# A row-wise maximum norm: the first tail tile loaded as 8192 + 8192 columns instead of 12672 + 3712

## The chip, the cores and the metric

The kernel runs on one core of one Trainium2 chip. The metric is the device time of one execution in microseconds (us). TensorE is not used; the work is done by transfers from the chip's memory (16 DMA engines of the core, fed from the queue that SyncE, SP, issues into) and by VectorE (DVE in the profile), which reduces.

## The reference

```python
x = np.random.randn(8192, 8192).astype(np.float32)

def reference(x):
    return np.linalg.norm(x, ord=np.inf, axis=1)
```

For a matrix and `axis=1` this is the vector norm of every row: the largest absolute value in each of the 8192 rows. The input is 268 MB of float32, the output 8192 numbers. Every element is read once and takes part in one maximum.

## The kernel before, in words

**Tiles.** A tile in the on-chip memory has 128 partitions. Each partition holds two rows of the matrix that follow each other in memory, so 2 x 8192 = 16384 columns, 64 KB a partition and 8.4 MB a tile. The matrix makes 32 such tiles. The first 24 are the bulk, the last 8 the tail. Three buffers (`BUFS = 3`) go round: tile n is loaded into the buffer that tile n - 3 leaves. A buffer is released as a whole, when the last reduction that reads it has ended.

**Bulk (lines 300 to 307).** Each tile is one load on SP's queue and one reduction on VectorE, which takes the maximum of absolute values over each of the two rows and writes two numbers a partition to `r_bulk`. VectorE's instruction is issued from the helper `absmax` (line 296), so all reductions stand under L296 in the profile; they are told apart by the tile written: `r_bulk`, `part`, `t` or `r_tail`.

**Tail, first seven tiles (lines 309 to 320).** Here a tile is loaded in several pieces, so that VectorE can begin on a piece while the next is still coming. The table `TAIL` (line 18) gives the widths of the pieces, tile by tile; they are counted from 0 here, so that "tile 0" is the first line of `TAIL`, "tile 3" the fourth. The widths are written out by hand. `segments` (line 39) cuts the pieces at the end of a row, since a reduction has one row's maximum as its result: a piece that runs over the border between the two rows at column 8192 gets two reductions. Each reduction writes one number a partition to `part`, in the next free column of its row; `part` has room for three a row (`k_max`, line 283) and is set to zero by POOL at the start. For tile 0 the pieces 12672 and 3712 give three reductions: columns 0 to 8192 (row 0), 8192 to 12672 (4480 columns of row 1), both after the first load, and 12672 to 16384 (3712 columns of row 1) after the second.

**The last tile (lines 327 to 358).** It is loaded in twelve pieces (`LAST`, line 29) that get narrower, reduced one by one; one reduction over all of `part` (192 ns in the profile) makes the results of the first seven tail tiles in between. The bulk's results are stored from ScalarE's queue, those of the tail from SP's.

**What sets the order.** All loads are issued by SP in the order of the program (lines 303, 315, 341), each as soon as its buffer is free; there are eight completion semaphores, used in turn, so a load also waits until the load eight before it has landed. The DMA engines work through the queue in order. VectorE runs its reductions in the order of the program, each waiting for the load that it reads. Some functions at the end of the program take out waits that are implied by others, issue the first load ahead of the start, and close the program from POOL (lines 52 to 248); the change does not touch them.

Of the kernel before, what the change touches and what calls it, by code (L numbers as in the profile page):

```python
# [15 lines left out]


TAIL = [
    [12672, 3712],
    [4992, 11392],  # L20
    [7040, 9344],
    [9344, 7040],
# [372 lines left out]
```

## Time and profile before

| what | value |
|---|---|
| device time, three runs | 627.03, 626.57, 627.04 us; median 627.03 us |
| profiled execution, first to last instruction (span) | 624.1 us |
| last store of the profiled execution lands, from the span's start | 624.7 us |
| instructions | 151, of these 63 reductions on VectorE |
| VectorE busy | 552.4 us, 89% of the span |
| the load queue's packets, share of 16 DMA engines | 99.7% |
| bytes read | 268.44 MB, 430 GB/s over the span |

The profiled execution has no device time of its own beside its span; the three runs' median stands 2.9 us above the span.

How to read it: the span is the time from the first to the last instruction of one profiled execution, and all times of instructions and landings are counted from its start. "Busy" is the time in which an engine worked; "idle before" is the time that it stood still ahead of a group of instructions, and "<-" names what ended the wait. A load's "landing" is the moment at which all of it has arrived. Reductions overlap at their ends: the next one's start is recorded some 0.08 us before the end of the one in front, so what a reduction costs VectorE is read from start to start, not from its own duration.

In the tail the trace has, in us from the span's start:

| load of tail tile | columns | issued | landed | its first reduction starts |
|---|---|---|---|---|
| 0, first | 12672 | 445.24 | 481.59 | 483.82 |
| 0, second | 3712 | 445.61 | 485.97 | 497.14 |
| 1, first | 4992 | 464.55 | 491.89 | 501.06 |
| 1, second | 11392 | 464.92 | 505.38 | 506.32 |
| 2, first | 7040 | 483.93 | 513.70 | 518.31 |
| 2, second | 9344 | 484.30 | 524.70 | 525.70 |
| 3, first | 9344 | 501.18 | 535.73 | 535.75 |
| 3, second | 7040 | 501.55 | 544.11 | 545.61 |
| 6, first | 4096 | 553.12 | 587.83 | 587.85 |
| last tile, twelfth | 768 | 611.38 | 622.19 | 622.34 |

The load ahead of tile 0's, of the last bulk tile, landed at 466.66, and that tile's reduction ran from 466.68 to 483.90.

### The profile page before, as it was taken

How to read it: one execution, taken by the hardware profiler on the slowest of the kernel's cores; microseconds unless marked ns; L12 is line 12 of the kernel's file. 1: busy time of each engine (PE TensorE's matmuls, PEld its weight loads, DVE VectorE, ACT ScalarE, POOL GpSimd, SP SyncE). 2: the span in 40 equal slices, each digit the busy share in tenths (PEclk: the TensorE clock that was granted, in tenths of full speed). 3: DMA queues.
4: the chain of work that ended last, by engine and by line, in shares of the span. 5: the costliest groups of instructions: out<-in, count | busy, mean ns of one | idle time of the engine just before them, and what ended most of it. 6: DMA issues, size and time to landing. Idle time of an engine off the chain costs nothing.

```text
span 624.1 us, 151 instructions
## 1 busy us (share of the span) xinstructions
DVE 552.4 (89%) x63; POOL 0.3 (0%) x5
## 2 busy tenths in 40 slices
DVE  0688988889988899888898888988889999999999
POOL 0000000000000000000000000000000000000000
DMA  9999999999999999999999999999999999999998
GB/s 403 470 403 454 420 428 445 403 470 403 470 403 441 433 403 470 403 470 403 470 403 470 403 462 412 437 437 403 470 434 397 440 448 422 422 437 430 429 427 354
DMA packets 8593, 268.47 MB, mean 430 GB/s; under 512 B 1424, under 2 KB 1424, under 8 KB 2832
## 3 DMA queue, kind: packets, MB, share of 16 engines
q1 hardware_dynamic: 8064, 268.44, 99.7%
q10 hardware_dynamic: 528, 0.02, 0.1%
q14 instruction: 1, 0.01, 0.0%
HBM read 268.44 MB, written 0.03 MB: 430 GB/s over the span
## 4 chain that ended last, share of the span: by engine, by line
DMA 63%; DVE 36%; another core or an unknown queue 0%; DVEq 0%; issue 0%
DMA t<-in_x_dram 63%; DVE r_bulk L296 25%; DVE part L296 8%; DVE t L296 3%; DVEq L390 0%; DVE r_tail L296 0%
## 5 line engine op out<-in xcount | busy, mean ns | idle before, releaser
L296 DVE TENSOR_REDUCE r_bulk<-t 128x2 f32<-128x16384 f32 x24 | 413.3, 17220 | 70.6 <-DMA t<-in_x_dram 70.6
L296 DVE TENSOR_REDUCE part<-t 128x1 f32<-128x8192 f32 (+19 forms) x26 | 121.3, 4741 | 0.3
L296 DVE TENSOR_REDUCE t<-t 128x1 f32<-128x1792 f32 (+7 forms) x10 | 16.3, 1692 | 0.0
L296 DVE TENSOR_REDUCE r_tail<-t 128x1 f32<-128x772 f32 (+1 forms) x2 | 1.8, 948 | 0.0
L296 DVE TENSOR_REDUCE r_tail<-part 128x14 f32<-128x42 f32 x1 | 0.2, 192 | 0.0
L293 POOL MEMSET part<- 128x42 f32 x1 | 0.1, 133 | 0.0
L379 POOL MEMSET const-bfloat16-1.0<- 128x1 bf16 x1 | 0.1, 101 | 0.0
L379 POOL MEMSET const-uint8-127<- 128x1 uint8 x1 | 0.1, 101 | 0.0
L379 POOL MEMSET const-float32-0.0<- 128x1 f32 x1 | 0.1, 98 | 0.2 <-issue 0.2
L379 POOL MEMSET const-float32-1.0<- 128x1 f32 x1 | 0.1, 98 | 0.0
## 6 DMA issues: line engine op xcount, KB each, us to landing
t<-in_x_dram SPq DMA_DIRECT2D x2, 4672.0 KB, 37.5
t<-in_x_dram SPq DMA_DIRECT2D x2, 3520.0 KB, 36.2
t<-in_x_dram SPq DMA_DIRECT2D x1, 6336.0 KB, 36.3
t<-in_x_dram SPq DMA_DIRECT2D x1, 5696.0 KB, 40.5
t<-in_x_dram SPq DMA_DIRECT2D x2, 1792.0 KB, 34.3
t<-in_x_dram SPq DMA_DIRECT2D x1, 3392.0 KB, 37.5
t<-in_x_dram SPq DMA_DIRECT2D x1, 3008.0 KB, 44.2
t<-in_x_dram SPq DMA_DIRECT2D x1, 2496.0 KB, 27.3
```

The source lines that it names most:

```text
L293: nc.gpsimd.memset(part[:], 0.0)
L296: return nc.vector.reduce_max(out=o, in_=i, axis=X, apply_absolute_value=True)
L379: nc = _bacc.Bacc("TRN2", target_bir_lowering=False, num_devices=1)
```

## The change

```diff
 TAIL = [
-    [12672, 3712],
+    [8192, 8192],
     [4992, 11392],
     [7040, 9344],
     [9344, 7040],
     ...
```

Tile 0 of the tail is still loaded in two pieces, but each is now exactly one row of the two. `segments` therefore makes one reduction of each piece, two instead of three: columns 0 to 8192 after the first load, 8192 to 16384 after the second. The 4480- and 3712-column reductions of row 1 become one of 8192. Row 1 of this tile now fills one column of `part` instead of two; the others stay at the zero that POOL wrote. Everything else in the program is as before: the other tiles' pieces, the number and order of the loads, the buffers, and the size of `part`.

## The prediction

> **What bounds the kernel now.** I read the page first (busy shares, queues), then the chain that ended last, then the busy time by stage, then the groups with shapes kept apart, then single stretches of the order of time.
>
> From the page:
> ```profile
> span 624.1 us, 151 instructions
> DVE 552.4 (89%) x63; POOL 0.3 (0%) x5
> q1 hardware_dynamic: 8064, 268.44, 99.7%
> L296 DVE TENSOR_REDUCE r_bulk<-t 128x2 f32<-128x16384 f32 x24 | 413.3, 17220 | 70.6 <-DMA t<-in_x_dram 70.6
> L296 DVE TENSOR_REDUCE part<-t 128x1 f32<-128x8192 f32 (+19 forms) x26 | 121.3, 4741 | 0.3
> ```
> The load queue's packets fill 99.7% of what 16 DMA engines have in the span: the transfers are the bound. VectorE idles 70.6 us, all of it in the bulk, waiting for loads; in the tail it idles 0.3 us before the part reductions. The table by stage says the same (start:end, length, DVE busy, POOL busy, clock, DMA share, GB/s):
> ```profile
> 466.66:483.90 17.24, 17.22 (x2) 0.00 (x0) 1.00 0.95 410
> 483.82:535.70 51.88, 51.82 (x10) 0.00 (x0) 1.00 1.01 435
> 535.70:587.85 52.15, 51.95 (x12) 0.00 (x0) 1.00 1.00 431
> ```
> From 483.82 us on both are full: VectorE has no gap to speak of and the DMA engines none at all. So the question is which of the two decides, and the chain (start, us, what) answers:
> ```profile
> 466.68 17.22 DVE r_bulk L296
> 483.90 17.26 DVE part L296 x3
> 501.16 0.02 issue
> 501.18 34.55 DMA t<-in_x_dram
> 535.73 0.02 issue
> 535.75 17.35 DVE part L296 x3
> 553.10 0.02 issue
> 553.12 34.71 DMA t<-in_x_dram
> 587.83 0.02 issue
> 587.85 17.52 DVE part L296 x6
> ```
> The three part reductions of 483.90 to 501.16 are those of the tile that changes. Twice behind them VectorE is held by a landing: at 535.73 (first load of tile 3) and at 587.83 (first load of tile 6). The last load lands at 622.19 in the trace, and VectorE starts its last reduction at 622.34.
>
> **The change, part by part.**
>
> *VectorE, tile 0.* Removed: the reductions of 4480 and 3712 columns. Added: one of 8192. From the groups with shapes apart (count, busy, mean ns, idle):
> ```profile
> L296 DVE TENSOR_REDUCE part<-t 128x1 f32<-128x8192 f32 x4 | 34.7, 8681 | 0.1
> L296 DVE TENSOR_REDUCE part<-t 128x1 f32<-128x4480 f32 x1 | 4.8, 4810 | 0.0
> L296 DVE TENSOR_REDUCE part<-t 128x1 f32<-128x3712 f32 x1 | 4.0, 4012 | 0.0
> ```
> Busy time: 4810 + 4012 - 8681 = 141 ns less. On the path it is less than that, as the order of time shows:
> ```profile
> 492.41 8.74 DVE L296 TENSOR_REDUCE part<-t 128x1 f32<-128x4480 f32 x2
> 497.14 9.27 DVE L296 TENSOR_REDUCE part<-t 128x1 f32<-128x3712 f32 x2
> ```
> The 4480 starts at 492.41 and ends 4.81 later, at 497.22; the 3712 has started at 497.14, 0.08 before that, and ends at 501.15; the next starts at 501.06. From start to start the tile takes 501.06 - 483.82 = 17.24 us. An 8192 takes 492.41 - 483.82 = 8.59 from start to start, so two take 17.18: 0.06 us saved. The Trainium skill, VectorE: DVE Perf Modes, section "The DRAIN you can't avoid", has a next operation start only when the pipe of the one before is empty, which would make the whole 0.14 us the saving; the starts here overlap the ends, so the trace does not agree, and by either number the sum below is the same, since the next wait takes it.
>
> *Where the 0.06 goes.* Behind tile 0 each reduction starts 0.06 earlier while its load has landed: tile 1's second load lands at 505.38 and is wanted at 506.32, tile 2's second lands at 524.70 and is wanted at 525.70; both have over 0.9 us to spare. At tile 3 VectorE is free at 535.64 and already waits 0.11 us, for the landing of 535.73. That landing is set by the DMA queue, not by VectorE (next parts), so the wait grows to 0.17 and all that follows starts when it did. Gain at the end: 0.00.
>
> *The transfers.* Two loads before, two after, the same 8 MB, the same 256 packets, issued at the same places on SP (445.24 and 445.61 us, behind the release by the third-last bulk reduction). No packet of 32768 bytes is in the trace. Its neighbours: 28160 bytes took 1044 ns and 37376 took 1382 ns, on a straight line 1213 ns for 32768; a pair takes 2426 ns. The old pair took 1872 (50688 bytes) + 554 (14848) = 2426 ns: no difference, times 8 packets on each of 16 engines. Measured from landing to landing, the old pair took 14.93 + 4.37 = 19.31 us (466.66 to 485.97). Bounds from other tail loads: at the best rate among them (4736 columns, 435.6 GB/s) the new pair takes 19.26, 0.05 less; at that of the nearest slower one (7040 columns, 430.0 GB/s) 19.51, 0.20 more; at the worst of all (1152 columns, 406.8 GB/s) 20.62, 1.31 more. I take 0.00, because packet times lie on a line to the nanosecond and 8192 lies between 7040 and 9344, and keep -0.05 to +0.20 for the range; the worst row is a load a seventh as long, and serves as the price of a rival. Since the queue never empties, a delay here would move every later landing, and the end, by as much.
>
> *When the data is wanted.* The first load now lands at about 466.66 + 19.31/2 = 476.3 instead of 481.59; it is wanted at 483.82, so the 2.2 us to spare become 7.5. The second lands at 485.97 as before; it was wanted by the third reduction at 497.14 and is now wanted by the second at 492.41: 6.4 us to spare instead of 11.2. This moved wait is the only one added; behind it on VectorE stands the whole tail, and it would cost only what the landing is late beyond 492.41. Without that cover a late microsecond is a microsecond at tile 1, up to the 0.11 that tile 3 absorbs.
>
> *The buffer.* Tile 3's loads wait for tile 0's last reduction: issued at 501.18, now 501.12. In between the queue holds loads that land up to 524.70, so 23 us of transfers hide the issue; 0.06 earlier or a few us later is nothing. If that cover were gone, the issue would be worth its full delay. SP issues the same number of loads in the same order, each waiting for the load eight before it; those of tile 0 are met by tile 4's at 518.42, long after either landing. The partials keep three columns a row because tile 6 still needs three, so neither POOL's clearing nor the 0.19 us reduction over all partials changes.
>
> Sum: 0.00 - 0.00. Against the profiled span of 624.1 us: 624.1. The runs' median of 627.03 is 2.9 above that span; kept, this gives 627.0.
>
> **The rivals.**
>
> *The saving arrives at the end.* If tile 3's and tile 6's loads landed a little earlier than in this profile, VectorE would have no wait behind tile 0 and end 0.06 earlier: 626.97. For it: the two waits were only 0.11 and 0.15 us. Against it: the last load lands at 622.19, and VectorE's last reduction cannot start before. The bigger 0.14 gives 626.89. Either lies within 0.2% (1.25 us), which is about what a measurement of this kernel can tell from no change.
>
> *Slower: the two even loads run below the rate of their neighbours.* Place: 466.66 to 485.97 on the load queue. It decides, beyond 0.2%, once the pair takes 20.56 us, that is below 408 GB/s. At the worst row's 406.8 it is +1.31: 628.3. For it: no load of this length was seen, both now start at a row's start, and nothing absorbs a delay of a full queue. Against it: the bulk and every long tail load stand at 430 to 435.
>
> *Slower: the queue runs dry before tile 3.* That needs its issue to slip from 501.18 to beyond 524.70; the release would have to be 23 us later, and two reductions end no later than three. Each us beyond would cost one; a slip of 25 would give 628.5.
>
> *Faster by over 0.2%.* Only the transfers could give it: the pair in 18.05 us, at 465 GB/s, above every row. With that: 625.8.
>
> **How the numbers follow.** The saving absorbed: 0.68, 627.0. The saving arriving, at least in part: 0.18, 626.9 to 627.0. Slower by the rate: 0.07, by a dry queue: 0.02. Faster: 0.05. So same 0.86, faster 0.05, slower 0.09. The range: the lowest run less 0.05 (rate) and 0.06 (saving) is 626.46, the highest plus 0.20 is 627.24; as three runs do not bound a median, half their spread of 0.47 goes on either side: 626.2 to 627.5. This holds the first two cases, 0.86; the others lie outside.
>
> **What the changed profile would show.** 150 instructions, DVE x62 with about 552.3 us; six part reductions of 8192 columns; tile 1's first start at about 501.00; the landing of tile 0's first load near 476.3, of its second near 486.0, of tile 3's first near 535.7; the idle before 535.75 at 0.17 instead of 0.11; the last landing at 622.2; span 624.0 to 624.1. The absorption is wrong if the start after 535.7 moves with the saving. The forecast as a whole is wrong if the second landing is not near 486.0, or if the queue's share falls below 99.7% because engines sit idle between 485 and 536 us.

## The result and the profile after

The changed kernel takes 627.34 us (median of 21 runs, 627.00 to 627.72), the kernel before 626.56 us beside it (21 runs, 626.33 to 627.04). The ratio is 1.0013, with a 95% interval of 1.0007 to 1.0019: a small loss, 0.78 us, that the runs tell apart from no change.

The page of the changed kernel, the lines that answer to those shown of before:

```profile
span 624.3 us, 150 instructions
DVE 552.4 (88%) x62; POOL 0.3 (0%) x5
q1 hardware_dynamic: 8064, 268.44, 99.7%
q14 instruction: 1, 0.01, 0.0%
L296 DVE TENSOR_REDUCE part<-t 128x1 f32<-128x8192 f32 (+17 forms) x25 | 121.2, 4925 | 0.3 <-DMA t<-in_x_dram 0.2
L296 DVE TENSOR_REDUCE r_tail<-t 128x1 f32<-128x772 f32 (+1 forms) x2 | 1.9, 954 | 0.3 <-DVE r_tail L296 0.3
```

The transfers are as before. New is the last line: 0.3 us of idle time ahead of one of the two reductions that close the kernel, and it is not a load that ends it. The chain that ended last (start, us, what) shows where:

```profile
483.80 17.19 DVE part L296 x2
500.99 0.02 issue
501.01 34.62 DMA t<-in_x_dram
535.63 0.02 issue
535.65 17.35 DVE part L296 x3
...
587.74 17.52 DVE part L296 x6
...
621.20 0.17 issue
621.37 0.96 DVE r_tail L296
622.33 0.26 issue
622.59 0.96 DVE r_tail L296
```

Tile 0 now takes two reductions, and the landing of tile 3 still starts the next stretch at 535.65. From there on everything stands 0.10 us earlier than in the profile of before, because this execution's bulk was 0.10 us earlier. The last load landed at 622.08 (before: 622.19) and VectorE's wait for it ended at 622.13 (622.24). But the last reduction started at 622.59 (622.34): 0.46 us behind its wait, where it had been 0.10. In order of time (start, us, engine, what, idle before):

```profile
619.25 2.20 DVE L296 TENSOR_REDUCE t<-t 128x1 f32<-128x1024 f32 x2
621.37 0.95 DVE L296 TENSOR_REDUCE r_tail<-t 128x1 f32<-128x772 f32 x1
622.59 0.96 DVE L296 TENSOR_REDUCE r_tail<-t 128x1 f32<-128x774 f32 x1 [0.27 <-DVE r_tail L296]
```

The reduction named as the releaser had ended at 622.32, and all that the last one reads was there at 622.13. So the wait of 0.27 us is for something that the program does not show. The page has one line that may belong to it: that of queue q14, one packet of 8 KB in the span, of the kind `instruction`, and so an instruction fetch. In the trace of before that packet goes out at 622.47, while the last reduction runs; in the changed kernel at 623.76, 1.17 us after the last reduction started. So packet and reduction both come later, but it is not this packet that the reduction waited for.

### The profile page after: what moved, and what is told of

Read it like the earlier page. It is cut to its first block, busy times and chain, and to the rows that moved or that the text cites. A ratio compares the mean times of both kernels' runs of the same rounds, so it can differ in the third digit from the quotient of the medians.

```text
span 624.3 us, 150 instructions
## 1 busy us (share of the span) xinstructions
DVE 552.4 (88%) x62; POOL 0.3 (0%) x5
## 4 chain that ended last, share of the span: by engine, by line
DMA 63%; DVE 36%; another core or an unknown queue 0%; issue 0%
DMA t<-in_x_dram 63%; DVE r_bulk L296 25%; DVE part L296 8%; DVE t L296 3%; DVE r_tail L296 0%
## 5 line engine op out<-in xcount | busy, mean ns | idle before, releaser
L296 DVE TENSOR_REDUCE part<-t 128x1 f32<-128x8192 f32 (+17 forms) x25 | 121.2, 4925 | 0.3 <-DMA t<-in_x_dram 0.2
```

The lines of the kernel that those rows point to most:

```text
L296: return nc.vector.reduce_max(out=o, in_=i, axis=X, apply_absolute_value=True)
```

## The experiments

Some words used below: a reduction is *held* when it starts later than all that it waits for would explain, its *gap* is the idle time that this leaves ahead of it, and a *filler* is a small reduction that is added and whose result nothing reads. *Beyond the span* is the device time of a run less its span.

The idea after this look was **theory P, place**: neither the loads nor the tail's reductions cost the time; VectorE's closing instructions moved one place forward in its instruction stream, and a fixed place of that stream is held back. **Rival L, loads**: the even loads cost it. **Rival W**: the shorter tail or its waits. **Rival T**: the size of the whole program.

### The loads alone, the reduction alone

Loads even, but row 1 reduced in its two old pieces:

```diff
     segs = [segments(loads, cols) for loads in TAIL]
+    segs[0] = [(0, 0, 0, 8192), (1, 1, 0, 4480), (1, 1, 4480, 3712)]
```

> Tile 0 loaded as 8192 + 8192, but row 1 still reduced in two pieces (4480 and 3712), so VectorE has the 63 reductions of the kernel before. Theory P (what counts is where VectorE's closing instructions stand in its stream, which lost one instruction ahead of them): as the kernel before, 626.56 us, ratio 1.0000 within 0.0005; the last reduction starts about 0.1 us after the wait on the last landing, as before, not 0.46 us. Rival L (the even loads cost it): as the changed kernel, 627.34 us, ratio 1.0013.

Measured: 626.47 us, ratio 0.9992 (0.9983 to 1.0001). No gap.

Loads as before, row 1 of tile 0 reduced by one instruction:

```diff
     [12672, 3712],
 ...
+    segs[0] = [(0, 0, 0, 8192), (1, 1, 0, 8192)]
```

> Tile 0 loaded as 12672 + 3712 as before, but row 1 reduced by one instruction of 8192 that waits for both loads: VectorE has 62 reductions, the loads are those of the kernel before. Theory P: as the changed kernel, 627.34 us, ratio 1.0013, last reduction held some 0.3 us longer than its data. Rival L: as the kernel before, 626.56 us.

Measured: 627.66 us, ratio 1.0011 (1.0002 to 1.0019), with the gap:

```profile
621.60 0.95 DVE L297 TENSOR_REDUCE r_tail<-t 128x1 f32<-128x772 f32 x1
622.82 0.96 DVE L297 TENSOR_REDUCE r_tail<-t 128x1 f32<-128x774 f32 x1 [0.27 <-DVE r_tail L297]
```

So the loss goes with the missing reduction and not with the loads: rival L falls. (The kernel before was itself slower in this measurement, 626.90 us; more on that under "What stays open".)

### An instruction given back, one too many

One small reduction in the bulk, where VectorE waits 2 us for each load; `spare` is a name for the unused tile `gap` of the kernel:

```diff
             nc.sync.dma_start(out=t[:, :W], in_=x_b[a, n])
+            if a == 0 and n in (3,):
+                absmax(spare[:, n : n + 1], t[:, :128])
```

> The changed kernel with one small reduction more (128 columns, into a column that nothing reads) ahead of the fourth bulk tile's reduction, where VectorE waits 2 us for a load anyway; 63 reductions on VectorE again, tail untouched. Theory P: the loss goes, 626.56 us, ratio 1.0000 within 0.0005. Rival L, and rival W (the tail's shorter reductions or their waits cost it): 627.34 us, ratio 1.0013. Any theory without the stream's length gives no gain, as this only adds work.

Measured: 626.54 us, ratio 0.9995 (0.9986 to 1.0004). The two closing reductions follow each other again:

```profile
620.40 1.08 DVE L296 TENSOR_REDUCE t<-t 128x1 f32<-128x896 f32 x1
621.39 1.82 DVE L296 TENSOR_REDUCE r_tail<-t 128x1 f32<-128x772 f32 x2
```

More work, put 540 us ahead of the end, and the loss is gone. Rival W falls with it, since the tail is that of the changed kernel. The same reduction added to the kernel before, which makes 64:

> The kernel before with the same small reduction in the bulk: 64 reductions. Rivals L and W: 626.56 us, since VectorE waits there 2 us for a load. Theory P: the closing instructions move one place the other way; either nothing (626.56) or a loss of the same kind (up to +0.8 us), to be read from the gap ahead of the last reduction.

Measured: 627.18 us, ratio 1.0006 (0.9997 to 1.0015). By time alone that is not clear of no change, but the trace has a gap. Now the first of the two closing reductions is held, 0.45 us behind its wait instead of 0.17:

```profile
621.77 1.82 DVE L296 TENSOR_REDUCE r_tail<-t 128x1 f32<-128x772 f32 x2 [0.20 <-DVE t L296]
```

With 62 the second is held, with 64 the first, with 63 neither. Between the two stands VectorE's wait for the last landing. Counted with that wait as an instruction of its own, it is the same place of the stream both times; with 63 reductions the wait stands there, and no hold shows, by theory P because it ends before the load does.

### Other numbers: 61, 65, 66, 86

61: the changed kernel, and tile 3's row 1 in one reduction.

```diff
+    segs[3] = [(0, 0, 0, 8192), (1, 1, 0, 8192)]
```

> The changed kernel, and in tile 3 row 1 is reduced by one instruction that waits for that tile's second load (landing 544.1, VectorE there at 544.3): 61 reductions. Theory P, sharpened by the first four runs: VectorE is held some 0.3 us at one fixed place of its stream, the place just ahead of the last reduction of the 63-reduction kernel, where that kernel has a wait for the last landing, which hides it; and an instruction-fetch packet of queue q14 is sent when it reaches the place two behind that last reduction. With 61 reductions the held place is the branch behind the last reduction: no gap ahead of either closing reduction, span 623.9 to 624.1; the fetch comes only after VectorE's last instruction of the span, so the time beyond the span is the longest, at least the 3.0 of the changed kernel: 627.0 to 627.6, ratio 1.0005 to 1.0015. Rival 'even is slow' (62 and 64 were slow, 63 fast): 61 is fast, ratio 1.0000 or less. Rival 'only 63 is fast': gap of 0.2 to 0.3 ahead of one of the last two reductions.

Measured: 627.55 us, ratio 1.0017 (1.0008 to 1.0026); median span 623.9 beside 623.8 of before, and 3.60 us beyond the span instead of 2.62. As expected there is no gap, and nearly all of the loss lies beyond the span:

```profile
621.29 1.81 DVE L297 TENSOR_REDUCE r_tail<-t 128x1 f32<-128x772 f32 x2
```

The hold is in this trace all the same, one instruction further on: the one instruction DRAIN that the end of the program puts on VectorE (line 391) starts at 622.54, 0.39 us after the last reduction (622.16). In the traces with 62 and 63 reductions it starts at most 0.05 us behind the last reduction's start, in the kernel before at 622.32 with the reduction at 622.34. So the held place fits with 61 too, but here nothing of the span waits for it.

The last store shows where the time went (issues of the last microseconds: KB, us from issue to landing). First the kernel with 61, then the changed kernel measured a second time (below), then the kernel with one filler, 63:

```profile
out_dram<-r_tail SPq DMA_DIRECT2D x1, 8.0 KB, 2.4
```

```profile
out_dram<-r_tail SPq DMA_DIRECT2D x1, 8.0 KB, 2.1
```

```profile
out_dram<-r_tail SPq DMA_DIRECT2D x1, 8.0 KB, 1.4
```

The store of 8 KB takes 1.41 to 1.42 us with 63 to 66 reductions and 1.64 to 2.44 us with 62 and 61. (With 86 it took 1.58 us, though no fetch was near, so not all of its scatter has this source.) In the trace 15 of its 16 engines land as always; one is late, by 0.22 us in the changed kernel (624.997 and 625.219) and by 1.02 with 61 (624.556 and 625.573). In these kernels the fetch packet goes out at 623.6 to 624.1, ahead of or among the store's own packets at 624.0 to 625.1, and takes 0.5 to 1.1 us; with 63 and 64 it goes out at 622.1 to 622.5, when the loads are done and the store is still to come. That the fetch is what makes the one engine late is argued from these times; the trace does not say which engine carried it. The device time follows the store: in the thirteen profiled executions of this study whose device time is known, it is the store's landing plus 1.94 to 1.96 us in twelve and 1.99 in one.

Three, four and 24 small bulk reductions added to the changed kernel:

```diff
+            if a * G + n in (3, 4, 5):
+                absmax(spare[:, a * G + n : a * G + n + 1], t[:, :128])
```

> The changed kernel with three small reductions ahead of three bulk reductions: 65 reductions, tail untouched. Theory P: the held place is the wait for the landing before the last one (621.25), which hides it; fetch packet at about 622.3 or earlier; no gap, ratio 0.9990 to 1.0000. Rival 'even is slow': also fast. Rival 'only 63 is fast': slow, ratio 1.0006 or more.

> The changed kernel with four small bulk reductions: 66. Theory P: the held place is the 896-column reduction of the last tile, which has no wait ahead of it on its own; VectorE is behind there by at most the 0.3, and the last landing at 622.1 to 622.2 gives back part: end later by 0 to 0.2 us, ratio 0.9992 to 1.0005. Rival 'even is slow': ratio 1.0006 to 1.0013, with a gap ahead of one of the last two reductions.

> The changed kernel with one small reduction ahead of each of the 24 bulk reductions, in the 2 us that VectorE waits there: 86 reductions. Theory P: the held place and the fetch packet lie some 23 instructions ahead of the end, among the tail's first reductions, hidden by the queue of waits; no gap at the end, no fetch packet near 622 to 624; ratio 0.9985 to 1.0000, the fastest of all if the late fetch costs anything at the end. Rival 'even is slow': ratio 1.0006 or more. Rival 'each instruction more costs': slower than with one filler.

Measured: 627.11, 627.16 and 627.12 us; ratios 1.0010 (1.0001 to 1.0019), 1.0011 (1.0002 to 1.0020) and 1.0009 (1.0000 to 1.0018). No gap at the end and 2.64 to 2.66 beyond the span, as theory P has it, but its times are wrong: it expected ratios of 1.0000 at most for 65 and 86 and of 1.0005 at most for 66. The median spans are 624.4 to 624.5 beside 623.8. The rival "even is slow" falls, because 61 and 65 are slow. "Only 63 is fast" expected 65 to be slow, and as a statement of times it fits every kernel here; the gap ahead of a closing reduction, by which it was to be known, is missing with 61 and with 65, 66 and 86. So these three have a loss of another kind. VectorE waits in the tail, and what ends the wait is a load (65 reductions):

```profile
583.99 8.29 DVE L296 TENSOR_REDUCE part<-t 128x1 f32<-128x3456 f32 x2
592.89 13.19 DVE L296 TENSOR_REDUCE part<-t 128x1 f32<-128x3584 f32 x5 [0.61 <-DMA t<-in_x_dram]
```

In the half microsecond from 591.4 to 591.9 of the same kernel the queue of fetches has its packet:

```profile
q14 instruction: 1, 0.01, 3.9%
```

It went out at 591.51 in the middle of the full load queue. It took 0.31 us, and the load's packet that starts as it ends 1002 ns where the others of its size take 479. That makes one engine 0.83 us late, and a load has landed only when the last engine is done: of the last load 15 engines' parts are there at 622.21, the sixteenth at 622.83. Counted from the last bulk landing, tile 6's second load landed at 126.20 instead of 125.42 us and the last load at 156.15 instead of 155.53. With 66 reductions the packet goes out at 586.49 and the last load lands at 156.18; with 86 at 470.44 and 155.98.

### Is it VectorE's stream?

POOL's clearing of the partials in two instructions instead of one, which makes the changed kernel 151 instructions long again (the function that moves the clearing ahead of the program, `clear_partials_early`, is changed to move both; not shown):

```diff
-    nc.gpsimd.memset(part[:], 0.0)
+    nc.gpsimd.memset(part[:, : n_tail // 2], 0.0)
+    nc.gpsimd.memset(part[:, n_tail // 2 :], 0.0)
```

> The changed kernel with POOL's one clearing of the partials written as two instructions: the program has 151 instructions again, but VectorE still 62 reductions. Theory P (place in VectorE's own stream): no help, ratio 1.0009 to 1.0016, a gap of 0.27 ahead of the last reduction, time beyond the span 3.05. Rival T (the size of the whole program decides, on whatever engine): as the kernel before, ratio 1.0000, no gap.

Measured: 627.49 us, ratio 1.0015 (1.0005 to 1.0024), gap 0.28 us. Rival T falls.

A small reduction written behind the last one:

```diff
     nc.sync.dma_start(out=out_t, in_=r_tail[:])
+    absmax(spare[:, 0:1], t[:, :128])
```

> The changed kernel with one small reduction (128 columns, result not read) on VectorE behind the last one, with nothing waiting for it: 63 reductions, but the closing two stand where they stand in the changed kernel. Theory P splits its two terms: the gap of 0.27 ahead of the last real reduction stays (span about 624.1 to 624.4), the fetch packet comes while VectorE still drains, as with 63, so the time beyond the span falls from 3.05 to about 2.65: 626.8 to 627.0, ratio 1.0004 to 1.0009. Rival 'the number 63 decides': ratio 1.0000, no gap. Rival 'the added work costs, nothing moves': ratio 1.0013 or more.

Measured: 626.68 us, ratio 1.0003 (0.9994 to 1.0012), no gap. This is not the test that it was meant to be: the trace has the added reduction at 607.55, where the program's ordering moved it, and so ahead of the closing ones. As one more ahead of them it agrees with theory P, and as well with "only 63 is fast"; the span is 0.15 us longer than before's (medians 624.1 and 623.95), as one would expect where VectorE has no idle time. An instruction really behind the last one was not tried.

The changed kernel again, and a filler in the 21st bulk tile instead of the fourth:

> The changed kernel itself, timed beside the others on the same chip. Every theory: ratio 1.0007 to 1.0019 as first measured; theory P: gap of 0.27 ahead of the last reduction, time beyond the span 3.05.

> The changed kernel with one small reduction ahead of the 21st bulk tile's reduction instead of the fourth's: 63 reductions. Theory P: only the number ahead of the closing instructions counts, not where the added one stands: ratio 0.9992 to 1.0003, no gap, 2.65 beyond the span. A rival in which the added instruction helps by its own place (an early shift of the first tiles): no help here, ratio 1.0010.

Measured: 627.45 us, ratio 1.0014 (1.0005 to 1.0023), for the first, and 626.50 us, ratio 0.9999 (0.9989 to 1.0008), for the second. Both ran in one measurement beside the kernel before: the loss is there again, and one filler takes it away. Of the two places tried in the bulk either will do.

All together (medians; "before" is the kernel before in the same measurement; the first row is the repeated measurement of the changed kernel):

| reductions | kernel | ratio | span (before) | beyond the span (before) | fetch packet at |
|---|---|---|---|---|---|
| 62 | changed | 1.0014 | 624.3 (623.95) | 3.15 (2.62) | 623.56 |
| 62 | POOL in two | 1.0015 | 624.3 (623.95) | 3.18 (2.62) | 624.06 |
| 62 | reduction alone | 1.0011 | 624.5 (624.3) | 3.09 (2.64) | 623.89 |
| 61 | tile 3 merged too | 1.0017 | 623.9 (623.8) | 3.60 (2.62) | 623.61 |
| 63 | loads alone | 0.9992 | 623.8 (624.3) | 2.61 (2.64) | 622.21 |
| 63 | one filler | 0.9995 | 623.9 (624.3) | 2.64 (2.64) | 622.43 |
| 63 | late filler | 0.9999 | 623.9 (623.95) | 2.62 (2.62) | 622.11 |
| 63 | one ahead of the last pieces | 1.0003 | 624.1 (623.95) | 2.62 (2.62) | 622.30 |
| 64 | before + filler | 1.0006 | 624.5 (624.3) | 2.63 (2.64) | 622.44 |
| 65 | three fillers | 1.0010 | 624.5 (623.8) | 2.66 (2.62) | 591.51 |
| 66 | four fillers | 1.0011 | 624.5 (623.8) | 2.64 (2.62) | 586.49 |
| 86 | 24 fillers | 1.0009 | 624.4 (623.8) | 2.64 (2.62) | 470.44 |

The changed kernel's loss is the sum of two terms, each of which another kernel has nearly alone: 0.35 us in the span, where the trace has the held reduction (64 has this one, 0.2 in the span and nothing beyond), and 0.53 beyond it, where the trace has the late engine of the store (61 has this one, 0.98 beyond the span and 0.1 in it). Together they are the 0.87 us between 627.45 and 626.58.

**What stays open.** The runs show which place is held and when the packet goes out; why a place is held for some 0.3 us, and why from 65 reductions on the packet goes out some thirty microseconds and more ahead of the end, they do not. The hold is not a wait for the packet that the trace shows: with 62 and with 64 it goes out 0.7 to 1.5 us after the held reduction has started. That the packet is VectorE's is argued from its moving with VectorE's number of instructions and not with POOL's. All that was added or taken away on VectorE were reductions; another kind of instruction was not tried. The Trainium skill, Runtime: NRT & Kernel Launch, section "Instruction fetch mechanics", tells that an engine's instructions come in blocks of 16 KiB and that crossing into the next is mostly hidden. The packets here have 8192 bytes, and of the numbers tried it was hidden with 63 reductions alone. Also open: in the measurement of the first four kernels, the kernel before had a span of 624.3, some 0.4 us more than in the two that followed, which ran on another chip. There, both profiled kernels with the old loads show eight packets of tile 1's first load at 486.4 to 486.9 that took 1.0 to 1.3 us instead of 0.74, and both with the even loads do not. Whether the loads or the chip make them is open: the profile of before, with the old loads, has no such packets, and in the two that followed every profiled kernel had the even ones. So the ratios below 1 of that measurement are no gain to count on.

No kernel here is clearly faster than the kernel before. The change with one small reduction given back is as fast as the kernel before.

## Why the prediction was wrong

*VectorE, tile 0: right.* Tile 0 takes 17.18 us from start to start (483.71 to 500.89), as worked out. The part reductions of 8192 columns are now five, one more than the four of before; the prediction's six was a miscount on which nothing rests. And the section of the Trainium skill that it names, VectorE: DVE Perf Modes, "The DRAIN you can't avoid", goes on to say that a next operation that is not held (as that page uses the word) starts earlier; so the overlapping starts are no case against that section.

*Where the 0.06 goes: right.* The wait ahead of tile 3 is 0.18 us (predicted 0.17; 0.11 before), and the stretch behind it starts with the landing. Nothing of the saving arrives.

*The transfers: right.* A packet of 32768 bytes takes 1213 ns, the number read off the line between its neighbours; the pair takes 19.32 us (predicted 19.31). The loads landed at 476.22 and 485.87 (predicted 476.3 and 486.0), and from the last bulk landing to the last load it is 155.53 us in both kernels. The rival of a lower rate is wrong, and so is the queue that runs dry.

*The buffer: right.* Tile 3 was issued at 501.01 and landed at 535.63.

*The sum: wrong.* It ended with the last load, and took what follows from the kernel before: "The runs' median of 627.03 is 2.9 above that span; kept, this gives 627.0." The step that failed is this "kept", a term of nothing for all that comes after the last landing. Neither part of it was kept. The last reduction, whose start was expected 0.10 us behind its wait, started 0.46 behind it, and the time beyond the span grew by 0.45 to 0.56 in the kernels with 62 reductions. The step counted an instruction removed as time removed, and did not ask what stands behind it in VectorE's stream. The forecast of the end (0.86 for no change within 0.2%) names the size rightly and the sign not at all: the measured loss of 0.13% lies inside that bound, but it is a loss, and both slower rivals had other mechanisms.

*The number: luck.* That 627.34 lies near 627.0 and inside the range of 626.2 to 627.5 is no merit of the sum. The 2.9 set the median of three runs against the span of another execution; run by run in the experiments, what lies beyond the span of the kernel before is 2.6, and its median of 21 runs is 626.56. The forecast stood 0.47 us too high for a kernel with no change, and that hid more than half of the 0.78 that it left out. Nor is 0.2% about what a measurement can tell from no change: 21 runs told 0.13%.

The profile of before held one sign of it, which the prediction did not read: the page lists a packet of an instruction queue inside the span, and the trace has it at 622.47, 0.28 us behind the last landing and ahead of the store. That a packet stands there was to be seen; what a shift of it by one instruction would cost was not.

## What to carry to other kernels

An instruction removed from an engine moves all that stand behind it in that engine's stream. Where a kernel's end is a chain of waits of some tenths of a microsecond, look at where the instruction queue's packets fall: in a full load queue one went with a last landing 0.45 to 0.65 us later here, beside the last store with a landing 0.2 to 1.0 later, in the gap between them, with 63 reductions, with no loss. To tell such an effect from the change itself, give the instruction back somewhere harmless and see whether the time comes back.

## What the runs showed that was not expected

- A fetch of 8 KB among 268 MB of loads costs more than its own time: 0.31 us for itself, and 0.52 to 0.53 more for the load's packet that starts as it ends (1002 instead of 479 ns, 1144 instead of 611, 1744 instead of 1213). The last load lands 0.45 to 0.65 us later.
- The device time follows the landing of the last store, at 1.94 to 1.99 us behind it, more closely than the last instruction: kernels with the same span of 623.9 us took 626.5 and 627.55 us.
- A place in VectorE's stream was held for some 0.3 us. Nothing in the program's own dependencies showed it: the profile names the reduction in front as the releaser, which had ended 0.27 us before.
